# Attention scores issued in two groups instead of four, with the attention's and the gates' steps placed in other slots

## The chip, the cores and the metric

The kernel runs on one core of a Trainium2 chip. The time is device microseconds from launch to end on that core. The core has five engines that work from their own queues in program order: TensorE (PE in the profile; its weight loads are PEld), VectorE (DVE), ScalarE (ACT), GpSimd (POOL) and SyncE (SP), which issues most of the loads.

## The reference, cut to what matters

One decoder layer for a sequence of 256 positions of width 1024, all in float32:

```
proj  = x @ W_in                  -> [q | k | v | B | C | h | gate_attn | gate_conv]
y_att = causal attention(q, k, v) @ W_att      (8 heads of 64, rotary on the first 16 dims)
y_cnv = (B * causal_dwconv3(C * h)) @ W_cnv
mix   = (sigmoid(g_att) * y_att + sigmoid(g_cnv) * y_cnv) @ W_o
x     = LayerNorm(alpha * x + mix)
u     = causal_dwconv3(x @ W_up);  f = (silu(u_gate) * u_val) @ W_down
x     = LayerNorm(alpha * x + f)
```

With 256 positions there is one key block, so the block-sparse attention is plain causal attention over 256 keys. The change concerns the attention only, and the order in which it is mixed with the projections that come after q, k and v.

## The kernel before, in words

Each float32 operand is split into a high and a low part (fp32r), and a product is formed from three matmuls (high-high, high-low, low-high). Weights come as one packed stream: SyncE loads chunks of 1 MB into three buffers `raw`; ScalarE copies a unit of a chunk to its high part `wh` (`split_h`, L192) and VectorE subtracts it to get the low part `wl` (`split_l`, L197). There are nine buffers of each.

q, k and v come first. After them 22 units of weights for h, c, b (twice) and the 16 gates follow, two by two (`two_units`, L664). TensorE runs the wide part of each unit (`cols_wide`, L333: eight matmuls of 512 columns) and, after the second of a pair, the narrow parts of both (`cols_narrow`, L340: 16 matmuls of 256 columns). The result of each unit stands in one of four PSUM banks `acc`, in two halves that have to be summed: ScalarE copies one half to SBUF and VectorE adds the other (`conv_sum_act` L596 and `conv_sum_dve` L600 for h, c, b; `gate_sum_act` L648 and `gate_sum_dve` L652 for the gates).

The attention is spread over these units. Work of the attention and of the convolution is put beside unit `u` by `at(u, part, f)`, and `slot(u)` (L479) issues it: first the matmuls of the unit, then the lists "pe" and "act", then `split_h` of the weights five units ahead, `split_l` four units ahead, then the list "dve". Every engine keeps this order in its own queue, so an instruction that waits holds up all that stands behind it on its engine. `C0` is the first of these units (h); c starts at C0+2, b at C0+4, the second h, c, b at C0+6, C0+8, C0+10, and the gates at C0+12.

The steps for one pair of heads `p` (of four), with their slots before the change:

| step | what it does | slot |
|---|---|---|
| `scores` (L397, L405) | 12 matmuls q times k on half the array each (64 rows), the two heads side by side, into two PSUM banks `ps` | C0+4+3p |
| `masked` (L408, L413) | VectorE adds the mask, scales, and takes the row maxima; L416 negates them | C0+5+3p |
| `exps` (L419, L424) | ScalarE: four exponentials with row sums | C0+6+3p |
| `normalize` (L428) | VectorE: reciprocal and four products | C0+7+5p |
| `probs_T` (L436) | six transposes on TensorE into two banks `ps` | C0+8+5p |
| `probs_h`, `probs_l` (L445, L448) | ScalarE and VectorE split each head's result, a slot apart | C0+9+5p, C0+10+5p |
| `attend` (L451) | six matmuls with v; needs both parts of both heads from its second matmul on | C0+11+5p |
| `attend_h`, `attend_l` | split of the result | C0+12+5p |

There are four `ps` banks, used in turn by the transposes of q and k (`qk_transpose`, slot C0+2, read by `qk_h` and `qk_l` in C0+3), the scores, `probs_T` and `attend`. The masked scores have two buffers (tag "pr"), so pair 2 takes over that of pair 0 when pair 0's transposes are done. The convolution's steps `conv1` to `conv4` (L602 to L627) stand beside the units at L630.

Of the kernel before, what the change touches and what calls it, by code (L numbers as in the profile page):

```python
# [8 lines left out]
F32 = mybir.dt.float32  # L9
# [6 lines left out]
P = 128  # L16
# [4 lines left out]
HD = 64  # L21
# [116 lines left out]
def layer_kernel(ctx: ExitStack, tc: tile.TileContext, x, wpack, cpack, ln1_g, ln1_b, ln2_g, ln2_b, out):  # L138
    nc = tc.nc

    cst = ctx.enter_context(tc.tile_pool(name="cst", bufs=1))
    big = ctx.enter_context(tc.tile_pool(name="big", bufs=1))
# [10 lines left out]
    def ps_bank(name):  # L153
        return ps_pool.tile([P, 512], F32, tag="ps", name=name)

    def scratch(shape, name, bufs=None, tag="scr"):
        return tmp.tile(shape, F32, tag=tag, name=name, bufs=bufs or 6)
# [5 lines left out]
    chunks, plan_units, U = plan()  # L163
# [24 lines left out]
    def split_h(u):  # L188

        issue_dma(units[u]["chunk"] + RAW_BUFS - 1)  # L190
        alloc(u, "h", "wh")
        nc.scalar.activation(units[u]["h"], raw_of(u), AF.Copy)  # L192

    def split_l(u):

        alloc(u, "l", "wl")
        nc.vector.tensor_tensor(units[u]["l"], raw_of(u), units[u]["h"].bitcast(F32), op=ALU.subtract)  # L197
# [161 lines left out]
    qkT = big.tile([P, 2, KT, S], F32R, tag="b16", name="qkT")  # L359
# [34 lines left out]

    SB, SM, PR = {}, {}, {}

    def scores(p):  # L397

        SB[p] = [ps_bank(f"s{p}_{j}") for j in range(2)]
        for t in range(2):  # L400
            n = (t + 1) * P
            for a, b in ((0, 0), (0, 1), (1, 0)):
                for j in range(2):
                    hs = slice(j * HD, (j + 1) * HD)
                    nc.tensor.matmul(SB[p][j][:, t * 256:t * 256 + n], qkT[hs, a, p, t * P:(t + 1) * P],  # L405
                                     qkT[hs, b, 4 + p, 0:n], start=a + b == 0, stop=a == 1)

    def masked(p):  # L408
        st = tmp.tile([P, 16], F32, tag="st", name=f"st{p}", bufs=4)
        sm = scratch([P, 2, 384], f"sm{p}", tag="pr", bufs=2)  # L410
        for t in range(2):
            for j in range(2):
                nc.vector.tensor_tensor_reduce(  # L413
                    out=sm[:, j, PCOL[t]], in0=SB[p][j][:, t * 256:t * 256 + P * (t + 1)], in1=MASK[t], scale=SCALE,
                    scalar=-3.0e38, op0=ALU.add, op1=ALU.max, accum_out=st[:, 2 * t + j:2 * t + j + 1])
        nc.vector.tensor_scalar(st[:, 4:8], st[:, 0:4], -1.0, None, op0=ALU.mult)  # L416
        SM[p] = (sm, st)
# [56 lines left out]
    def at(u, part, f, *a):  # L474
        beside.setdefault(u, {}).setdefault(part, []).append((f, a))
# [3 lines left out]
    def slot(u, products=None):  # L479


        if products:
            products()
        mine = beside.pop(u, {})
        for f, a in mine.get("pe", []) + mine.get("act", []):
            f(*a)
        while done["h"] <= u + LA + 1:
            if units[done["h"]]["h"] is None:
                split_h(done["h"])
            done["h"] += 1  # L490
        while done["l"] <= u + LA:
            if units[done["l"]]["l"] is None:
                split_l(done["l"])
            done["l"] += 1
        for f, a in mine.get("dve", []):
            f(*a)
# [9 lines left out]
    C0 = U[(OFF_H, 0)]  # L506
    for t in range(2):
        at(C0 + t, "dve", rope, t)
    for g2 in (0, 2, 1, 3):
        at(C0 + 2, "pe", qk_transpose, g2)  # L510
        at(C0 + 3, "act", qk_h, g2)
        at(C0 + 3, "dve", qk_l, g2)
    for p in range(4):
        at(C0 + 7 + 5 * p, "dve", normalize, p)
    for p in range(4):
        s = C0 + 4 + 3 * p
        at(s, "pe", scores, p)
        at(s + 1, "dve", masked, p)
        at(s + 2, "act", exps, p)
        s = C0 + 7 + 5 * p  # L520
        at(s + 1, "pe", probs_T, p)
        for j in range(2):
            at(s + 2 + j, "act", probs_h, p, j)
            at(s + 2 + j, "dve", probs_l, p, j)
        at(s + 4, "pe", attend, p)
        at(s + 5, "act", attend_h, p)
        at(s + 5, "dve", attend_l, p)


    def x_split(k):  # L530
# [96 lines left out]
    def conv4_dve(pr):  # L627
        low(yT[:, 1, 2 * pr:2 * pr + 2, :], CB["t", pr], yT[:, 0, 2 * pr:2 * pr + 2, :])

    for pr, (c1, c2, c3, c4) in enumerate(((6, 10, 11, 13), (13, 16, 18, 21))):  # L630
        at(C0 + c1, "dve", conv1, pr)
        at(C0 + c2, "act", conv2_act, pr)
        at(C0 + c2, "dve", conv2_dve, pr)
        at(C0 + c3, "dve", conv3, pr)
        at(C0 + c4, "act", conv4_act, pr)
        at(C0 + c4, "dve", conv4_dve, pr)
        for nm, off in (("h", OFF_H), ("c", OFF_C), ("b", OFF_B)):
            for e in range(2):
                at(U[(off, pr)] + e + 2, "act", conv_sum_act, nm, pr, e)
                at(U[(off, pr)] + e + 2, "dve", conv_sum_dve, nm, pr, e)  # L640


    GB = {}
# [13 lines left out]
    for j in range(16):  # L657
        u = U[("g", 0)] + j
        at(max(u + 3, C0 + 17), "act", gate, j)
        at(u + 2, "act", gate_sum_act, j)  # L660
        at(u + 2, "dve", gate_sum_dve, j)


    def two_units(u, names):  # L664
        banks = []
        for e in range(2):
            banks.append(acc_bank(names[e]))
            slot(u + e, lambda: cols_pair(u + e, e == 1, banks, xT))
        return banks
# [9 lines left out]
    for e in range(2):  # L679
        slot(U[("g", 0)] + 16 + e)  # L680
# [20 lines left out]
    for half in range(2):  # L701
        for e in range(2):
            ua, uc = U[("ao", half)] + e, U[("co", half)] + e
            for n in range(2):
                i = half * 4 + e * 2 + n
                if i > 1:
                    mix_hl(i - 2)
                ahead(uc + n - 1)
                bank = ps_bank(f"y{i}")
                unit_cols(uc, bank[:, 256:512], yT[:, 0], yT[:, 1], n * P)  # L710
                unit_cols(ua, bank[:, 0:256], aT[:, 0], aT[:, 1], n * P)
                if i == 0:
                    slot(uc + n)
                mix(i, bank)
# [139 lines left out]
    rows = {}  # L854
# [191 lines left out]
```

## Time and profile before

| what | value |
|---|---|
| median of 3 runs | 368.86 us (368.48 to 370.68) |
| profiled execution, its own time | 369.0 us |
| its span, first to last instruction | 367.1 us |
| mean granted TensorE clock | 0.997 |
| busy: TensorE, VectorE, ScalarE, GpSimd | 358.0, 294.9, 217.0, 7.0 us |
| data read, share of the span's time | 68.24 MB, 189 GB/s with what is written |

The page gives each engine's busy time and the chain of work that ended last; the order of time (timeline) gives each engine's instructions with start and length in us, merged where equal ones follow each other, with the idle time before them and what ended it in brackets. A length reaches to the end of the last one; since instructions overlap at their ends, the distance between two starts is the better price of one step. In the chain, times of TensorE are those of the ends, some 0.1 us later than the starts in the order of time.

### The profile page before, as it was taken

Reading aid. Unit: us, or ns where it says so; the run is one execution under the profiler, and the core shown is the slowest. Engines: PE = TensorE matmul, PEld = TensorE weight load, DVE = VectorE, ACT = ScalarE, POOL = GpSimd, SP = SyncE. Lnnn points to the kernel's source line nnn. Section 1 sums busy time; section 2 is a strip of 40 time slices with the busy share of each in tenths; the row PEclk is TensorE's granted clock in tenths of the full one; section 3 lists DMA queues with packets and bytes.
Section 4 is the critical chain, followed back from the end, with each engine's and each line's share of the span. In section 5 each row is a group of like instructions: output and inputs, shape, how many; then the busy total and the mean of one; then the engine's idle time right before and its main releaser. Section 6 shows DMA issues by size and latency. Waiting matters only on the chain.

```text
span 367.1 us, 5335 instructions
## 1 busy us (share of the span) xinstructions
PE 358.0 (98%) x2022; PEld 312.2 (85%) x2022; DVE 294.9 (80%) x510; ACT 217.0 (59%) x372; POOL 7.0 (2%) x26
## 2 busy tenths in 40 slices
PE   8999999999999999999999999999999999999991
PEld 7888888888888899988888888888888888888891
DVE  4696887788895679869769988987869696999784
ACT  4685776747867654634266666575657566676300
POOL 2000000000000000102000000000000000000000
PEclk9999999999999999999999999999999999999998
DMA  7978565333853634596360835448182645662011
GB/s 263 356 292 318 180 225 211 114 114 129 331 214 130 221 124 137 190 357 224 124 223 12 341 121 221 153 193 309 46 334 90 254 140 204 228 237 108 0 59 57
DMA packets 11241, 69.63 MB, mean 190 GB/s; under 512 B 1232, under 2 KB 1616, under 8 KB 4176
## 3 DMA queue, kind: packets, MB, share of 16 engines
q1 hardware_dynamic: 10496, 67.00, 50.0%
q0 software_dynamic: 576, 2.10, 1.8%
q8 instruction: 16, 0.26, 0.3%
q10 hardware_dynamic: 144, 0.20, 0.1%
q14 instruction: 9, 0.07, 0.1%
HBM read 68.24 MB, written 1.05 MB: 189 GB/s over the span
## 4 chain that ended last, share of the span: by engine, by line
PE 97%; DVE 1%; DMA 1%; DVEq 0%; SPq 0%; issue 0%
PE pb L333 20%; PE pb L340 10%; PE g L333 8%; PE d L305 5%; PE d L306 5%; PE d L307 5%; PE g L340 4%; PE q L555 3%; PE k L555 3%; PE v L555 3%; PE b L333 2%; PE y L326 2%; PE y L325 2%; PE y L324 2%; PE c L333 2%; PE o L307 2%
## 5 line engine op out<-in xcount | busy, mean ns | idle before, releaser
L197 DVE TENSOR_TENSOR wl<-raw,wh 128x1024 fp32r<-128x1024 f32 x90 | 109.8, 1221 | 23.3 <-ACT wh L192 22.7
L192 ACT ACTIVATE wh<-raw 128x1024 fp32r<-128x1024 f32 x90 | 94.5, 1055 | 22.7 <-DMA raw<-in_wpack 22.6
L333 PE MATMUL pb<-x1T,wh 128*128 128x512 f32 x320 | 76.2, 390 | 0.0
L333 PEld LDWEIGHTS pb<-x1T,wh 128*128 128x128 f32 x320 | 59.7, 188 | 12.1
L220 DVE TENSOR_TENSOR wl<-raw,wh 128x1024 fp32r<-128x1024 f32 (+1 forms) x38 | 38.0, 1037 | 7.4 <-ACT wh L219 7.1
L340 PEld LDWEIGHTS pb<-x1T,wl 128*128 128x128 f32 x320 | 41.0, 191 | 1.6
L340 PE MATMUL pb<-x1T,wl 128*128 128x256 f32 x320 | 41.5, 283 | 0.0
L219 ACT ACTIVATE wh<-raw 128x1024 fp32r<-128x1024 f32 (+1 forms) x38 | 32.9, 904 | 14.3 <-DMA raw<-in_wpack 8.5
L333 PE MATMUL g<-xT,wh 128*128 128x512 f32 x128 | 31.4, 393 | 0.0
L305 PE MATMUL d<-wh,f 128*128 128x512 f32 x80 | 31.3, 391 | 0.0
L306 PE MATMUL d<-wl,f 128*128 128x512 f32 x80 | 31.3, 391 | 0.0
L307 PE MATMUL d<-wh,f 128*128 128x512 f32 x80 | 31.1, 389 | 0.0
L333 PEld LDWEIGHTS g<-xT,wh 128*128 128x128 f32 x128 | 23.3, 188 | 4.5
L807 ACT ACTIVATE fb<-pb 128x512 f32<-128x512 f32 x20 | 11.9, 595 | 23.8 <-PE pb L340 23.8
L825 DVE SCALAR_TENSOR_TENSOR fc<-fb,consts,fc 128x254 f32<-128x254 f32 x40 | 19.3, 484 | 1.4
L823 DVE SCALAR_TENSOR_TENSOR fc<-fb,consts,fc 128x255 f32<-128x255 f32 x40 | 19.1, 478 | 0.0
L817 ACT ACTIVATE fc<-fb,consts 128x256 f32<-128x256 f32 x40 | 17.9, 496 | 0.4 <-DVE fb L811 0.4
L307 PEld LDWEIGHTS d<-wh,f 128*128 128x128 f32 x80 | 15.0, 188 | 3.2
L305 PEld LDWEIGHTS d<-wh,f 128*128 128x128 f32 x80 | 15.1, 189 | 2.7
L306 PEld LDWEIGHTS d<-wl,f 128*128 128x128 f32 x80 | 15.1, 189 | 2.6
L340 PEld LDWEIGHTS g<-xT,wl 128*128 128x128 f32 x128 | 16.4, 191 | 0.6
L340 PE MATMUL g<-xT,wl 128*128 128x256 f32 x128 | 16.6, 283 | 0.0
(183 smaller groups left out, 606.1 us busy)
## 6 DMA issues: line engine op xcount, KB each, us to landing
raw<-in_wpack SPq DMA_DIRECT2D x55, 1024.0 KB, 4.9
raw<-in_wpack SPq DMA_DIRECT2D x6, 896.0 KB, 5.5
xr<-in_x SPq DMA_DIRECT2D x1, 1024.0 KB, 7.6
ln<-in_ln_g POOLq DMA_DIRECT2D x2, 512.0 KB, 5.6
ln<-in_ln_b POOLq DMA_DIRECT2D x2, 512.0 KB, 6.2
raw<-in_wpack SPq DMA_DIRECT2D x3, 256.0 KB, 3.4
raw<-in_wpack SPq DMA_DIRECT2D x1, 512.0 KB, 5.8
out<-x SPq DMA_DIRECT2D x2, 256.0 KB, 2.1
```

The costliest lines, as they stand in the source:

```text
L192: nc.scalar.activation(units[u]["h"], raw_of(u), AF.Copy)
L197: nc.vector.tensor_tensor(units[u]["l"], raw_of(u), units[u]["h"].bitcast(F32), op=ALU.subtract)
L219: nc.scalar.activation(h, src, AF.Copy)
L220: (eng or nc.vector).tensor_tensor(l, src, h.bitcast(F32), op=ALU.subtract)
L305: nc.tensor.matmul(o, ah, bh, start=start, stop=False)
L306: nc.tensor.matmul(o, ah, bl, start=False, stop=False)
L307: nc.tensor.matmul(o, al, bh, start=False, stop=stop)
L333: nc.tensor.matmul(bank, un["h"][:, k, :], b[:, k].rearrange("p a s -> p (a s)"), start=k == 0, stop=False)
L340: nc.tensor.matmul(bank[:, 0:S], un["l"][:, k, :], b[:, k, 0], start=False, stop=k == nk - 1)
L555: nc.tensor.matmul(banks[m][t], (xl if p == 2 else xh)[:, k, t * P:(t + 1) * P], wl if p == 1 else wh, start=k == 0 and p == 0, stop=k == ...
L823: nc.vector.scalar_tensor_tensor(c[:, 1:S], pb[:, a * S:a * S + S - 1], w_ffn(1, j), c[:, 1:S], op0=ALU.mult, op1=ALU.add)
L825: nc.vector.scalar_tensor_tensor(c[:, 2:S], pb[:, a * S:a * S + S - 2], w_ffn(0, j), c[:, 2:S], op0=ALU.mult, op1=ALU.add)
```

## The change

- `scores` takes a list of pairs and issues the matmuls of all of them in one group, first the query half t = 0 for each pair, then t = 1. Pairs 0 and 1 are issued in slot C0+4, pairs 2 and 3 in C0+9. The number and the shapes of the matmuls stay.
- The masked scores of pairs 2 and 3 stand in a tile of their own (`sm23`), which takes the place of q and k (tag "rows"), not in the two buffers of pairs 0 and 1.
- The slots of the steps are written out pair by pair: masked C0+5, 7, 10, 12; exps C0+6, 8, 11, 13; normalize C0+8, 14, 17, 21; probs_T C0+11, 15, 19, 23; probs_h and probs_l one and two slots after probs_T, attend three, attend_h and attend_l four. attend ends in slot C0+26, as before.
- `slot` has a new list "first", which it issues between `split_h` and `split_l`. `conv_sum_dve` and `gate_sum_dve` move into it from "dve", so that they stand ahead of the slot's `split_l` in VectorE's queue.
- conv2 of the first h, c and b moves from C0+10 to C0+9; of the second, conv1 moves from C0+13 to C0+14 and conv4 from C0+21 to C0+20.

```
--- before.py
+++ after.py
@@ -394,20 +394,24 @@
 
     SB, SM, PR = {}, {}, {}
 
-    def scores(p):
-
-        SB[p] = [ps_bank(f"s{p}_{j}") for j in range(2)]
+    def scores(ps):
+
+        for p in ps:
+            SB[p] = [ps_bank(f"s{p}_{j}") for j in range(2)]
         for t in range(2):
             n = (t + 1) * P
-            for a, b in ((0, 0), (0, 1), (1, 0)):
-                for j in range(2):
-                    hs = slice(j * HD, (j + 1) * HD)
-                    nc.tensor.matmul(SB[p][j][:, t * 256:t * 256 + n], qkT[hs, a, p, t * P:(t + 1) * P],
-                                     qkT[hs, b, 4 + p, 0:n], start=a + b == 0, stop=a == 1)
+            for p in ps:
+                for a, b in ((0, 0), (0, 1), (1, 0)):
+                    for j in range(2):
+                        hs = slice(j * HD, (j + 1) * HD)
+                        nc.tensor.matmul(SB[p][j][:, t * 256:t * 256 + n], qkT[hs, a, p, t * P:(t + 1) * P],
+                                         qkT[hs, b, 4 + p, 0:n], start=a + b == 0, stop=a == 1)
 
     def masked(p):
         st = tmp.tile([P, 16], F32, tag="st", name=f"st{p}", bufs=4)
-        sm = scratch([P, 2, 384], f"sm{p}", tag="pr", bufs=2)
+        if p == 2:
+            SM["late"] = big.tile([P, 2, 2, 384], F32, tag="rows", name="sm23")
+        sm = scratch([P, 2, 384], f"sm{p}", tag="pr", bufs=2) if p < 2 else SM["late"][:, p - 2]
         for t in range(2):
             for j in range(2):
                 nc.vector.tensor_tensor_reduce(
@@ -477,6 +481,7 @@
     done = {"h": 0, "l": 0}
 
     def slot(u, products=None):
+
 
 
         if products:
@@ -488,6 +493,8 @@
             if units[done["h"]]["h"] is None:
                 split_h(done["h"])
             done["h"] += 1
+        for f, a in mine.get("first", []):
+            f(*a)
         while done["l"] <= u + LA:
             if units[done["l"]]["l"] is None:
                 split_l(done["l"])
@@ -510,21 +517,20 @@
         at(C0 + 2, "pe", qk_transpose, g2)
         at(C0 + 3, "act", qk_h, g2)
         at(C0 + 3, "dve", qk_l, g2)
-    for p in range(4):
-        at(C0 + 7 + 5 * p, "dve", normalize, p)
-    for p in range(4):
-        s = C0 + 4 + 3 * p
-        at(s, "pe", scores, p)
-        at(s + 1, "dve", masked, p)
-        at(s + 2, "act", exps, p)
-        s = C0 + 7 + 5 * p
-        at(s + 1, "pe", probs_T, p)
+
+    at(C0 + 4, "pe", scores, (0, 1))
+    at(C0 + 9, "pe", scores, (2, 3))
+    for p, (m, e, n, tr, av) in enumerate(((5, 6, 8, 11, 14), (7, 8, 14, 15, 18), (10, 11, 17, 19, 22), (12, 13, 21, 23, 26))):
+        at(C0 + m, "dve", masked, p)
+        at(C0 + e, "act", exps, p)
+        at(C0 + n, "dve", normalize, p)
+        at(C0 + tr, "pe", probs_T, p)
         for j in range(2):
-            at(s + 2 + j, "act", probs_h, p, j)
-            at(s + 2 + j, "dve", probs_l, p, j)
-        at(s + 4, "pe", attend, p)
-        at(s + 5, "act", attend_h, p)
-        at(s + 5, "dve", attend_l, p)
+            at(C0 + tr + 1 + j, "act", probs_h, p, j)
+            at(C0 + tr + 1 + j, "dve", probs_l, p, j)
+        at(C0 + av, "pe", attend, p)
+        at(C0 + av + 1, "act", attend_h, p)
+        at(C0 + av + 1, "dve", attend_l, p)
 
 
     def x_split(k):
@@ -627,7 +633,7 @@
     def conv4_dve(pr):
         low(yT[:, 1, 2 * pr:2 * pr + 2, :], CB["t", pr], yT[:, 0, 2 * pr:2 * pr + 2, :])
 
-    for pr, (c1, c2, c3, c4) in enumerate(((6, 10, 11, 13), (13, 16, 18, 21))):
+    for pr, (c1, c2, c3, c4) in enumerate(((6, 9, 11, 13), (14, 16, 18, 20))):
         at(C0 + c1, "dve", conv1, pr)
         at(C0 + c2, "act", conv2_act, pr)
         at(C0 + c2, "dve", conv2_dve, pr)
@@ -637,7 +643,7 @@
         for nm, off in (("h", OFF_H), ("c", OFF_C), ("b", OFF_B)):
             for e in range(2):
                 at(U[(off, pr)] + e + 2, "act", conv_sum_act, nm, pr, e)
-                at(U[(off, pr)] + e + 2, "dve", conv_sum_dve, nm, pr, e)
+                at(U[(off, pr)] + e + 2, "first", conv_sum_dve, nm, pr, e)
 
 
     GB = {}
@@ -658,7 +664,7 @@
         u = U[("g", 0)] + j
         at(max(u + 3, C0 + 17), "act", gate, j)
         at(u + 2, "act", gate_sum_act, j)
-        at(u + 2, "dve", gate_sum_dve, j)
+        at(u + 2, "first", gate_sum_dve, j)
 
 
     def two_units(u, names):
```

## The prediction

> **What bounds the kernel now.** I read the page's busy shares first, then its chain, then the sums over two long stretches, and only then the order of time of TensorE, VectorE and ScalarE around the attention (38 to 100 us). From the page:
>
> ```profile
> PE 358.0 (98%) x2022; PEld 312.2 (85%) x2022; DVE 294.9 (80%) x510; ACT 217.0 (59%) x372; POOL 7.0 (2%) x26
> ...
> PE 97%; DVE 1%; DMA 1%; DVEq 0%; SPq 0%; issue 0%
> ```
>
> Two stretches that cover nearly the whole span (length, then busy time of each engine):
>
> ```profile
> 5.00:182.00 177.00, 177.00 (x1035) 154.88 (x1036) 140.80 (x266) 109.06 (x199) 3.95 (x6) 1.00 0.60 216
> 182.00:359.00 177.00, 177.00 (x957) 153.76 (x957) 148.60 (x233) 106.66 (x173) 0.55 (x1) 1.00 0.46 170
> ```
>
> TensorE is busy for 354 us without a hole, at a granted clock of 1.00. So two things alone can move the time: what TensorE itself needs, and a wait that comes new into its queue. A wait there is lost for good, since no hole later gives it back; time saved on another engine brings nothing.
>
> **What TensorE saves.** The change issues the same 48 score matmuls in two groups and not four. The chain shows a group with its neighbours (start, length), two pieces of a common block, and two early pieces for a rival below:
>
> ```profile
> 4.78 2.33 PE q L555 x6
> ...
> 13.94 1.36 PE q L555 x6
> ...
> 53.16 0.89 PE s L405 x12
> 54.04 2.05 PE b L333 x8
> ...
> 58.00 3.65 PE h L333 x16
> 61.66 1.91 PE h L340 x16
> ```
>
> A group costs 0.89, and the eight wide matmuls behind it take 2.05 where sixteen of h take 3.65, so eight 1.83: 1.11 in all. Inside a group the matmuls run two at a time. These rows of TensorE's order of time, from several narrow windows, show starts, each row with what is left of the group:
>
> ```profile
> 51.15 2.00 PE L333 MATMUL b<-xT,wh 128*128 128x512 f32 x8
> ...
> 53.36 0.56 PE L405 MATMUL s<-qkT 64*128 64x128 f32 x6
> ...
> 53.47 0.57 PE L405 MATMUL s<-qkT 64*128 64x256 f32 x6
> ...
> 53.97 2.12 PE L333 MATMUL b<-xT,wh 128*128 128x512 f32 x8
> ...
> 66.91 2.08 PE L333 MATMUL c<-xT,wh 128*128 128x512 f32 x8
> ...
> 77.43 0.40 PE L305 MATMUL av<-vpt 128*128 128x512 f32 x1
> ```
>
> Twos start 0.11 apart (53.36, 53.47). A second pair of heads in the same group adds six such steps, 0.66, in place of 1.11: 0.45 saved, twice, 0.90. Against it, the transposes of pair 1 stood just ahead of a score group and now stand ahead of wide matmuls, which are then 0.08 longer (66.91 against 51.15). Net -0.8. Bounds: no saving at all (0), and at most the entries and exits of all four groups (four times 0.45, 1.8); I take 0.8, as only two groups go.
>
> **What the re-spread order does to VectorE and ScalarE.** These are the rows that price it, VectorE first (a price is the distance to the next start where two rows follow each other):
>
> ```profile
> 47.49 2.47 DVE L216 TENSOR_TENSOR qkT<-qkt,qkT 128x512 fp32r<-128x512 f32 x4
> 49.88 0.41 DVE L600 TENSOR_TENSOR ch<-h,ch 128x256 f32<-128x256 f32 x1
> ...
> 71.50 0.55 DVE L216 TENSOR_TENSOR vpt<-ptp,vpt 128x384 fp32r<-128x384 f32 x1
> 71.97 1.91 DVE L617 SCALAR_TENSOR_TENSOR ct<-z,consts,ct 128x256 f32<-128x256 f32 x4
> 73.79 0.42 DVE L600 TENSOR_TENSOR cc<-c,cc 128x256 f32<-128x256 f32 x1
> 74.13 1.22 DVE L197 TENSOR_TENSOR wl<-raw,wh 128x1024 fp32r<-128x1024 f32 x1
> 75.26 0.28 DVE L413 CUSTOM_DVE_ANT_0 sm<-s,mask 128x128 f32<-128x128 f32 x1
> ...
> 76.49 0.17 DVE L416 TENSOR_SCALAR st<-st 128x4 f32<-128x4 f32 x1
> 76.56 0.68 DVE L622 TENSOR_TENSOR ct<-cb,ct 128x512 f32<-128x512 f32 x1
> 77.17 0.41 DVE L600 TENSOR_TENSOR cc<-c,cc 128x256 f32<-128x256 f32 x1
> ...
> 78.63 0.17 DVE L430 RECIPROCAL st<-st 128x4 f32<-128x4 f32 x1
> ...
> 79.76 0.85 DVE L216 TENSOR_TENSOR aT<-av,aT 64x256 fp32r<-64x256 f32 x2
> ```
>
> ```profile
> 48.21 0.41 ACT L596 ACTIVATE ch<-h 128x256 f32<-128x256 f32 x1
> ...
> 55.51 0.40 ACT L424 ACTIVATE sm<-sm,st 128x128 f32<-128x128 f32 x1 [1.27 <-DVE st L416]
> ...
> 57.28 0.36 ACT L596 ACTIVATE cb<-b 128x256 f32<-128x256 f32 x1
> 57.55 1.05 ACT L192 ACTIVATE wh<-raw 128x1024 fp32r<-128x1024 f32 x1
> 58.50 0.37 ACT L596 ACTIVATE cb<-b 128x256 f32<-128x256 f32 x1
> ...
> 70.22 0.47 ACT L446 ACTIVATE vpt<-ptp 128x384 fp32r<-128x384 f32 x1
> 70.59 0.90 ACT L611 ACTIVATE ct<-z,consts 128x256 f32<-128x256 f32 x2
> ...
> 82.59 0.62 ACT L625 ACTIVATE yT<-ct 128x512 fp32r<-128x512 f32 x1
> 83.11 0.37 ACT L596 ACTIVATE cb<-b 128x256 f32<-128x256 f32 x1
> ...
> 95.20 1.28 ACT L655 ACT_TABLE_LOAD   x1
> 96.50 1.31 ACT L655 ACTIVATE gates<-gs,consts 128x256 f32<-128x256 f32 x3
> ```
>
> Prices on VectorE: a sum (ch, cc, cb) 0.34, a low split wl 1.13, masked 1.30 (its maxima are ready 1.40 after its start), normalize 1.13, conv2 1.82, conv3 0.61, conv1 the same as an estimate (both are one 128x512 product), probs_l 0.47, the four qkT lows 2.39. On ScalarE: exps 1.77, a sum 0.27 (ready after 0.37), wh 0.95, conv4 0.52. For a handover between the two I allow 0.03.
>
> No piece of work is added, but the list "first" puts each sum ahead of the slot's low split on VectorE, and ScalarE does that sum behind the exponentials of its slot. So VectorE, which used to do a split and go on while ScalarE was in the exponentials, now stands at the sum until they are done; queued behind it are the splits, masked, normalize and probs_l. That makes a closed chain: masked(p), exps(p), ScalarE's sum, VectorE's sum, the next slots' work, masked(p+1). I follow it in the order that the built program shows.
>
> - Start: slot C0+3. The sum of ch waits for ScalarE until 48.62; then sum 0.34, wl 1.13, four qkT lows 2.39, two slots' sums and splits 2.94: masked(0) at 55.45.
> - Round 0: maxima 1.40, exps 1.77, sum 0.37, handovers 0.06: VectorE goes on at 59.05. Two sums, two splits, conv1: 3.55. masked(1) at 62.60.
> - Round 1: 3.60 more, 66.20. Three sums, three splits, normalize(0), conv2: 7.36. masked(2) at 73.56.
> - Round 2: 77.16. Two sums, two splits, conv3, probs_l(0,0): 4.02. masked(3) at 81.18.
> - Round 3: 3.60, and conv4 0.52 ahead of the sum: 85.30. Sum and split 1.47: probs_l(0,1) starts at 86.77 and ends at 87.32 (0.55).
>
> attend(0) needs that last one from its second matmul on. When is TensorE there? Wide matmuls resume behind the first group at 53.97 + 0.66 = 54.6; rest of the b block 2.05 + 1.91; h and c blocks 5.56 each (3.65 + 1.91): 69.7. The second group, 0.89 + 0.66: 71.3; the b block with its 0.22: 77.0; six transposes of 128 columns, 0.11 each like the scores' steps, and their 0.08: 77.8; g block 5.56, eight wide 1.83: 85.2; second matmul 0.23 (3.65 / 16) later, 85.4. So TensorE stands 87.3 - 85.4 = 1.9 us at slot C0+14. Before, the same probs_l ended at 72.05 and attend came at 77.43: 5.4 us of cover, which this order uses up.
>
> Next, attend(1): from its transposes to its second matmul TensorE has 0.66 + 0.08 + 5.56 + 1.83 + 0.23 = 8.4. The other side: first three transposes some 0.5 with their latency, then on ScalarE probs_h 0.37, conv2 0.8, sum 0.27, wh 0.95, probs_h 0.37, table load 1.3, three gates 1.31, sum 0.37, then VectorE's sum, split, probs_l 2.0: 8.2. About even; I take 0 and up to 0.5. attend(2) and (3) have neither table load nor conv2, so some 2 us of cover.
>
> **What costs nothing, and its cover.** The group of pairs 0 and 1 fills all four score banks, so its seventh matmul (the fourth two, at 53.47) needs the last qkT low, at 50.12 + 2.47 = 52.6: 0.9 of cover; beyond it TensorE would stand. The second group needs masked(1), at 64.0, by 69.7. The masked scores of pairs 2 and 3 stand where q and k were: q and k are read for the last time by the transposes, whose lows are done by 52.6, long before 73.6, and x1, which takes the place next, comes behind the last attend. The low splits come later, but with much in hand: C0+13's, for one, ends at 70.4 and is used from 77.8 + 3.65 = 81.4. SP's order is the same, but the buffers that its loads wait for come free with the later splits, the first at 50.2; a load takes 4.9:
>
> ```profile
> raw<-in_wpack SPq DMA_DIRECT2D x55, 1024.0 KB, 4.9
> ```
>
> It lands at 55.1, and ScalarE first reads it at 60.1 (exps from 56.9, two sums, one wh). Nothing of POOL's queue moves.
>
> **Sum.** -0.8 + 1.9 = +1.1 on the profiled execution (369.0), so 370.1; the median of the runs shown is 368.86, which gives 370.0.
>
> **Rivals.**
> - The cover holds (another engine's idle time takes it up): VectorE is idle for 36 us of the first stretch and ScalarE for 68. Then only the saving is left, 368.1. Against it: the chain above is made of waits for each other, not of busy time.
> - Slower by over 1%: the place is attend(1), where both sides are even. If the new waits for the sums lengthen each round between two attends, the stall comes again at attend(1) to (3). It decides from 3.7 + 0.8 = 4.5 us of stall in all, 2.6 more than I count, 0.9 for each of three; then 372.6 or more. Against it: the later rounds have no exponentials in them.
> - The stall costs clock too. The first six q matmuls, before which TensorE had stood, took 2.33 where later ones take 1.36: +1.0 if that happens again, so 371.0. The Trainium skill, TensorE: Matmul & The Clock Gate, section Part 1: The HAM clock gate, has the clock halved only after an idle window of about 3.4 us; by that rule this stall is too short, and no row of before shows a stall in the middle that would test it.
>
> **How the numbers follow.** A stall of 0.8 to 3.0 us: 0.70; the forecast is its 370.0, range 368.9 to 371.2 (the chain is 39 us of some forty instructions, and 3% on it is 1.2). Cover holds: 0.14. Clock lost: 0.06. Over 1%: 0.06. Unknown: 0.04. To leave out at most two in ten, the range reaches down to the case of full cover, and up past the clock's: 368.0 to 371.5. A difference within 1% is about what a measurement of this kernel cannot tell from no change; by these cases it is slower 0.06, faster 0.01, same 0.93.
>
> **What would show it.** In the profile after: score rows of 24 matmuls, about 1.6 long, two in number; TensorE idle once for some 1.7 us near 85.5, ended by VectorE's vpt row; VectorE idle in front of the sums, ended by ScalarE, near 46, 57, 64, 75 and 83. Right on time but with no idle TensorE, the chain is wrong; idle at attend(1) to (3) as well, the second rival. I am wrong altogether if the wide matmuls themselves start to wait for splits or banks.

## The result and the profile after

The median after is 371.37 us (369.72 to 372.34, 18 runs) against 368.78 us (368.12 to 370.68, 18 runs) for the kernel before on the same chip: a ratio of 1.0063 [1.0049, 1.0077]. The change makes the kernel slower by 0.6%. The forecast was 370.0 us, or 1.1 us more; 2.6 us came.

The page after, busy time and shares of the chain:

```profile
PE 357.6 (97%) x2022; PEld 311.5 (85%) x2022; DVE 293.4 (80%) x510; ACT 217.0 (59%) x372; POOL 7.0 (2%) x26
...
PE 84%; DVE 9%; ACT 3%; DMA 2%; issue 1%; SPq 1%; DVEq 0%
```

TensorE has the same work, but the chain that ends last now leaves it for VectorE and ScalarE. All waits of TensorE in the profile after (total, times, longest):

```profile
PE av L306 <- DVE vpt L216: 1.9, 1, 1.9
PE warm L234 <- DVE zeros L224: 1.0, 1, 1.0
```

The second row is the start and stands in both kernels. The first is the new one: attend's second matmul waits for the low part of the transposed probabilities (`probs_l`). The order of time of VectorE, ScalarE and TensorE after shows how it comes about:

```profile
48.14 0.43 DVE L606 TENSOR_TENSOR ch<-h,ch 128x256 f32<-128x256 f32 x1 [2.22 <-ACT ch L602]
...
54.94 0.28 DVE L417 CUSTOM_DVE_ANT_0 sm<-s,mask 128x128 f32<-128x128 f32 x1
...
58.53 0.42 DVE L606 TENSOR_TENSOR cb<-b,cb 128x256 f32<-128x256 f32 x1 [2.20 <-ACT cb L602]
...
62.08 0.28 DVE L417 CUSTOM_DVE_ANT_0 sm<-s,mask 128x128 f32<-128x128 f32 x1
...
73.05 0.28 DVE L417 CUSTOM_DVE_ANT_0 sm<-s,mask 128x128 f32<-128x128 f32 x1
...
80.66 0.28 DVE L417 CUSTOM_DVE_ANT_0 sm<-s,mask 128x128 f32<-128x128 f32 x1
...
84.78 0.42 DVE L606 TENSOR_TENSOR cb<-b,cb 128x256 f32<-128x256 f32 x1 [2.72 <-ACT cb L602]
...
86.25 0.55 DVE L216 TENSOR_TENSOR vpt<-ptp,vpt 128x384 fp32r<-128x384 f32 x1
```

```profile
83.37 0.49 ACT L428 ACTIVATE sm<-sm,st 128x256 f32<-128x256 f32 x1
...
83.86 0.61 ACT L631 ACTIVATE yT<-ct 128x512 fp32r<-128x512 f32 x1
84.39 0.36 ACT L602 ACTIVATE cb<-b 128x256 f32<-128x256 f32 x1
```

```profile
52.57 1.66 PE L407 MATMUL s<-qkT 64*128 64x128 f32 x24
54.16 2.12 PE L333 MATMUL b<-xT,wh 128*128 128x512 f32 x8
...
84.61 0.39 PE L305 MATMUL av<-vpt 128*128 128x512 f32 x1
86.86 0.50 PE L306 MATMUL av<-vpt 128*128 128x512 f32 x1 [1.86 <-DVE vpt L216]
87.19 0.40 PE L307 MATMUL av<-vpt 128*128 128x512 f32 x1
...
99.64 0.39 PE L305 MATMUL av<-vpt 128*128 128x512 f32 x1
100.02 0.50 PE L306 MATMUL av<-vpt 128*128 128x512 f32 x1
```

Read the last round backwards: probs_l at 86.25 stands behind a split (84.78 to 86.25 with the sum), the sum behind ScalarE's half of it at 84.39, and that behind the exponentials and conv4. VectorE stood idle for 2.72 us ahead of it; TensorE pays 1.86.

**A better ruler than the span.** This profiled execution took 370.07 us, only 1.1 more than the one of before, but that mixes two things: its first h matmul started at 37.74, before's at 38.26. Between executions of one kernel this start wanders (37.3 to 40.6 in those recorded here). From the first y matmul on all kernels agree: 57.56 to 57.67 us to the next block and 180.3 from there to the end. So I compare the stretch from the first h matmul to the first y matmul, which holds the whole attention. The rows show the stretch, its length and the busy time of TensorE, its loads, VectorE, ScalarE and GpSimd; before, after, and a later execution of after:

```profile
38.26:129.27 91.01, 91.01 (x561) 79.71 (x560) 73.43 (x158) 64.06 (x133) 0.00 (x0) 1.00 0.52 186
```

```profile
37.74:130.43 92.69, 90.83 (x562) 79.58 (x560) 70.80 (x156) 64.04 (x134) 0.00 (x0) 1.00 0.47 171
```

```profile
37.78:132.00 94.22, 92.37 (x561) 80.75 (x560) 70.79 (x156) 63.99 (x134) 0.00 (x0) 0.98 0.47 168
```

The stage grew by 1.68 us in the first profile and by 3.21 in the other, the same kernel, at a granted clock of 0.98 in place of 1.00. So there were two questions: which part of the change makes the wait, and where the second 1.5 us come from.

### The profile page after: what moved, and what is told of

It is laid out like the page before. It is cut to its first block, busy times and chain, and to the rows that moved or that the text cites. A ratio compares the mean times of both kernels' runs of the same rounds, so it can differ in the third digit from the quotient of the medians.

```text
span 368.3 us, 5318 instructions
## 1 busy us (share of the span) xinstructions
PE 357.6 (97%) x2022; PEld 311.5 (85%) x2022; DVE 293.4 (80%) x510; ACT 217.0 (59%) x372; POOL 7.0 (2%) x26
## 4 chain that ended last, share of the span: by engine, by line
PE 84%; DVE 9%; ACT 3%; DMA 2%; issue 1%; SPq 1%; DVEq 0%
PE pb L333 20%; PE pb L340 10%; PE g L333 6%; PE d L305 5%; PE d L306 5%; PE d L307 5%; PE g L340 4%; DVE wl L197 3%; PE k L561 3%; PE v L561 3%; PE q L561 2%; PE y L326 2%; PE y L325 2%; PE y L324 2%; PE o L307 2%; PE o L306 2%
## 5 line engine op out<-in xcount | busy, mean ns | idle before, releaser
L817 DVE TENSOR_TENSOR fb<-pb,fb 128x512 f32<-128x512 f32 x20 | 13.7, 686 | 3.7 <-ACT fb L813 3.5
```

## The experiments

Theories. A: the list "first" alone makes the wait, because VectorE's sum then stands in front of the splits while ScalarE's half of that sum stands behind the exponentials. B: the new slots or the grouped scores make it. For the rest, C: the wait costs clock as well; D: something else in the changed order is slower. The kernel before had these medians on the same chips: 369.02 us beside the first four runs, 368.88 beside the next four, 369.36 (one run) beside the last three.

**The changed kernel again** (no edit).

> The changed kernel once more, unaltered, with a second profile. My theory: in every execution TensorE stands about 2.0 us in the attend of pair 0 (2.02 in the first profile, with 0.11 behind it) and 0.2 to 0.3 in that of pair 1, which less the 0.8 saved in the score groups gives +1.6 between the q, k, v stage and the end. The runs lie further above the kernel before than that (medians 371.37 and 368.78, 2.6 apart), and spread more (369.7 to 372.3 against mostly 368.1 to 369.5). Theory for the rest: after the stall some executions lose clock for a while; then slow runs show a lower granted clock (0.988) and a profile that falls on one shows matmul steps of about 0.43 us for 512 columns behind the stall. Rival for the rest: the stall itself is longer in some executions, with the clock unchanged; then a second profile shows more than 2.0 us at the same place.

371.93 us (369.87 to 372.78), ratio 1.0061 [1.0039, 1.0084]: the result repeats. Two of its 11 runs lie below 370.4; in the first comparison it was 6 of 18 below 370.7, and the other 12 at 371.0 to 372.3. The profiled execution (370.99) had a stage of 92.67 and the whole clock, but a late start (38.68).

**The sums back behind the splits**, everything else of the change kept:

```
-                at(U[(off, pr)] + e + 2, "first", conv_sum_dve, nm, pr, e)
+                at(U[(off, pr)] + e + 2, "dve", conv_sum_dve, nm, pr, e)
...
-        at(u + 2, "first", gate_sum_dve, j)
+        at(u + 2, "dve", gate_sum_dve, j)
```

> The changed kernel with the sums back in the list dve, behind the slot's split and attention work; groups of scores, slots and the buffer stay. My theory (the sums ahead of the splits make VectorE wait for the exponentials, and this wait reaches the attend of pair 0): no idle TensorE in the attends, probs_l of pair 0 done by about 82, 3 us ahead of TensorE; the 0.8 saved in the score groups is left, so about 368.0, ratio 0.998 to the kernel before. Rival (the re-spread slots themselves, with masked and exps of pair 3 just ahead of probs_l of pair 0, cost the time): TensorE still stands 1 to 2 us there, 369.5 to 371.

368.12 us (367.27 to 370.07), ratio 0.9974 [0.9956, 0.9991]. This version beats both kernels. VectorE's and TensorE's order of time and the stage:

```profile
80.67 0.55 DVE L216 TENSOR_TENSOR vpt<-ptp,vpt 128x384 fp32r<-128x384 f32 x1
```

```profile
84.46 0.39 PE L305 MATMUL av<-vpt 128*128 128x512 f32 x1
84.69 0.39 PE L306 MATMUL av<-vpt 128*128 128x512 f32 x1
```

```profile
37.59:127.83 90.24, 90.24 (x561) 79.70 (x560) 73.86 (x158) 64.53 (x134) 0.00 (x0) 1.00 0.52 187
```

probs_l is done at 81.2, 3.5 us before TensorE needs it. The stage is 0.77 shorter than before's: that is the grouped scores with nothing against them. B is out: the new slots and the groups make no wait.

**The list "first" alone, in the kernel before.**

```
+        for f, a in mine.get("first", []):
+            f(*a)
         while done["l"] <= u + LA:
...
-                at(U[(off, pr)] + e + 2, "dve", conv_sum_dve, nm, pr, e)
+                at(U[(off, pr)] + e + 2, "first", conv_sum_dve, nm, pr, e)
...
-        at(u + 2, "dve", gate_sum_dve, j)
+        at(u + 2, "first", gate_sum_dve, j)
```

> The kernel before with one part of the change alone: the sums issued ahead of the slot's low split on VectorE. Score groups, slots and buffers as before. My theory: the sum stands behind the exponentials here too; worked through with the same prices TensorE comes to stand some 0.4 us at the transposes of pair 1 (their normalize ends near 84.4, where TensorE is at 84.0) and 1.6 to 1.8 us at the attend of pair 1, 2 us in all: 370.8, ratio 1.005. Rival (only the re-spread slots cost the time): same as before, 368.8, with no idle TensorE.

371.94 us (371.7 to 374.47), ratio 1.0083 [1.0055, 1.0111]: the list alone makes the kernel slower, also with the old slots. TensorE's waits there, and one of VectorE's ahead of a sum:

```profile
PE av L306 <- DVE vpt L216: 1.4, 1, 1.4
...
PE ptp L440 <- DVE sm L434: 0.7, 1, 0.7
```

```profile
84.14 0.42 DVE L602 TENSOR_TENSOR cb<-b,cb 128x256 f32<-128x256 f32 x1 [2.74 <-ACT cb L598]
```

The wait at attend, there that of pair 1, was expected; the one of pair 2's transposes for normalize was not, and the time came out 1.1 us above the 370.8 expected. The stage is 94.20 in that execution, at a granted clock of 1.00: the list costs 3.19 there. By TensorE's starts, counted from the first h matmul, 0.55 of it arises at pair 1's transposes and the scores behind them (0.4 was expected), 1.69 at the attend of pair 1 and 0.95 at pair 2's transposes. With the new slots and groups the list costs 2.45 (92.69 without clock loss, against 90.24 without the list). So the new slots don't cause the harm; by these profiles they ease it a little.

**The list kept, but ScalarE's half of the sum ahead of the exponentials.**

```
-        for f, a in mine.get("pe", []) + mine.get("act", []):
+        for f, a in mine.get("sum", []) + mine.get("pe", []) + mine.get("act", []):
...
-                at(U[(off, pr)] + e + 2, "act", conv_sum_act, nm, pr, e)
+                at(U[(off, pr)] + e + 2, "sum", conv_sum_act, nm, pr, e)
```

> The changed kernel, with ScalarE's copies for the sums of h, c and b issued ahead of the slot's exponentials and probs_h, not behind them; VectorE's sums stay ahead of the low splits. My theory (VectorE's sum costs time only because ScalarE's half of it stands behind the exponentials): probs_l of pair 0 done near 82, no idle TensorE in the attend of pair 0, about 368.0, ratio 0.997 to the kernel before, like the run with the sums last. Rival (a sum ahead of the split is harmful by itself): TensorE still stands 1 us or more there, 370 or more.

368.16 us (367.7 to 370.08), ratio 0.9985 [0.997, 1.0]. attend's first two matmuls start at 85.08 and 85.31 without a wait; probs_l is done before:

```profile
82.58 0.55 DVE L216 TENSOR_TENSOR vpt<-ptp,vpt 128x384 fp32r<-128x384 f32 x1
```

VectorE's sum may stand first; what hurts is that it waits for an instruction that its producer does last. A is shown from three sides: taken away, alone, and with the producer moved. A little of the harm stays: the stage is 90.52, 0.28 more than with the sums last. This version moved the sums of h, c and b only. The gates' sums still stand as in the changed kernel, one of them waits ahead of the last probs_l of pair 1, and the second matmul of attend(1) comes 0.38 behind the first (97.96 to 98.34) and not 0.23:

```profile
96.26 0.42 DVE L658 TENSOR_TENSOR gs<-g,gs 128x256 f32<-128x256 f32 x1 [0.37 <-ACT gs L654]
```

**Four score groups in the changed kernel**, in slots C0+4, 5, 9 and 10.

```
-    at(C0 + 4, "pe", scores, (0, 1))
-    at(C0 + 9, "pe", scores, (2, 3))
+    for p, c in enumerate((4, 5, 9, 10)):
+        at(C0 + c, "pe", scores, (p,))
```

> The changed kernel with the scores in four groups again, in slots C0+4, C0+5, C0+9 and C0+10. My theory: the stall ends at a time set by VectorE and ScalarE, so 0.9 us more of TensorE work ahead of it only shortens the stall, from 2.0 to about 1.1; the time stays within 0.3 us of the changed kernel. Rival (TensorE's work and its stall add up): 0.9 us slower than the changed kernel, with the stall at 2.0.

370.29 us (369.83 to 372.88), ratio 1.0046 [1.0025, 1.0066]. TensorE and the stage:

```profile
85.56 0.39 PE L305 MATMUL av<-vpt 128*128 128x512 f32 x1
87.03 0.50 PE L306 MATMUL av<-vpt 128*128 128x512 f32 x1 [1.08 <-DVE vpt L216]
```

```profile
37.90:130.58 92.68, 91.59 (x562) 79.67 (x560) 70.84 (x156) 64.29 (x133) 0.00 (x0) 1.00 0.47 171
```

TensorE is busy for 0.76 longer than after, it waits 0.78 less, and the stage is as long (92.68 against 92.69). The saving of the groups is real and is wholly given back as waiting, because VectorE's chain, which ends the wait, doesn't get shorter. So far this is as expected, but the median is 1.6 us below that of the changed kernel in the same comparison (371.93), where at most 0.3 was expected: 7 of 10 runs lie at 369.8 to 370.3. So the longer wait costs something that the same stage length in these two profiles does not show. That points to C: all ten runs have a mean granted clock of 0.992 to 0.996, while 4 of the 11 of the changed kernel have 0.988 to 0.991.

**A longer wait**: VectorE writes one low split once more, and in a second kernel three times more, ahead of the late probs_l.

```
+    def low_again(u):
+        nc.vector.tensor_tensor(units[u]["l"], raw_of(u), units[u]["h"].bitcast(F32), op=ALU.subtract)
+
+    for _ in range(1):
+        at(C0 + 13, "dve", low_again, C0 + 16)
```

> The changed kernel with one low split done twice on VectorE (the same unit, the same values), just ahead of the last probs_l of pair 0. It lengthens TensorE's stall by 1.13, from 2.0 to about 3.2 us. Theory of a stall that costs its length and no more: about 1.1 us over the changed kernel, its fast group at 371.2 where that of the changed kernel is at 370.1, granted clock as there. Theory that the stall costs clock in some executions: more of them lose it, a median 1.5 to 2.5 us over the changed kernel's, clock 0.988 in most, and matmul steps of 0.43 us for 512 columns behind the stall in the profile.

> The same with three splits more: a stall of 2.0 + 3.4 = 5.4 us. Theory of a stall that costs its length: 3.4 over the changed kernel, fast group at 373.5, clock as there. Theory that it costs clock: every execution loses a further 1.5 to 1.7 us, about 375.2 and more, and the profile shows the 0.43 us steps behind the stall.

One split more: 373.27 us (371.01 to 374.79), ratio 1.0117 [1.0087, 1.0148]. Three: 375.29 us (374.67 to 375.9), ratio 1.0176 [1.0151, 1.0202]. The waits became 3.0 and 5.5. The first one's profile, TensorE alone (stretch, length, busy, granted clock, share of DMA, GB/s):

```profile
84.00:88.07 4.07, 1.79 (x8) 1.00 0.00 0
88.07:94.90 6.83, 6.12 (x18) 0.50 0.43 154
94.90:98.00 3.10, 3.10 (x24) 1.00 0.80 314
```

From 88.07 on, before the wait ends (at 88.78), the granted clock is 0.50 for 6.83 us. With three splits it was 3.41 us. So a wait in the middle can cost clock, and a longer one doesn't cost proportionately more. Not every execution pays: of the six runs with one split more, five have a mean granted clock of 0.984 to 0.991 and take 372.9 to 374.8 us, and the sixth has 0.996 and takes 371.0, which is what was expected of a wait that costs its length alone (371.2).

**The changed kernel, four more profiled executions**, to see whether its own wait does that.

> The changed kernel unaltered, for one more profile. Theory of lost clock: if this execution is one of those at 371 or more with TensorE started as early as in the first profile, matmuls behind the stall of pair 0's attend take 0.43 us for 512 columns for some 1 to 3.4 us; if it is one at 370, they do not. Rival: a longer stall than 2.0 us.

> The changed kernel unaltered, one of three more looks. The longer stall of 3.0 us has shown half clock behind it (6.8 us of it); the changed kernel's own stall of 1.9 us has not in three profiles, of executions at 370.1, 370.3 and 371.0, while most executions lie at 371 to 373. Theory of lost clock: a look that falls on an execution of 371.6 or more with a normal start shows a stretch at half clock behind the stall, 0.43 us per 512 columns; a look at about 370 shows none. Rival: such an execution has the full clock there, and the time is lost elsewhere, in the start or in a longer stall.

> The changed kernel unaltered, the second of three more looks; as for the first.

> The changed kernel unaltered, the third of three more looks; as for the first.

370.27, 371.14, 371.72 and 371.99 us. The first has the wait (1.86) and no loss, and a stage of 92.64. The other three have the same wait (1.85) and a stage of 94.20 to 94.24. The order of time of TensorE in the execution of 370.27, then the same and the granted clock around the wait in that of 371.72:

```profile
87.10 0.50 PE L306 MATMUL av<-vpt 128*128 128x512 f32 x1 [1.86 <-DVE vpt L216]
...
88.01 2.02 PE L333 MATMUL g<-xT,wh 128*128 128x512 f32 x8
```

```profile
84.65 0.39 PE L305 MATMUL av<-vpt 128*128 128x512 f32 x1
86.89 0.50 PE L306 MATMUL av<-vpt 128*128 128x512 f32 x1 [1.85 <-DVE vpt L216]
...
87.93 3.46 PE L333 MATMUL g<-xT,wh 128*128 128x512 f32 x8
```

```profile
84.26:87.67 3.41, 1.56 (x8) 1.00 0.16 24
87.67:91.09 3.42, 3.42 (x11) 0.50 0.70 283
91.09:95.00 3.91, 3.91 (x30) 1.00 0.45 140
```

Eight wide matmuls that took 2.02 in the execution without loss take 3.46 here: for 3.41 us the clock is half. The stage is 1.55 longer for it. This is C, in the changed kernel itself; D has nothing left to explain in these profiles.

The mean granted clock of the other runs says how often it happens. 3.41 us at half clock lower the mean of a run of 370 us by 0.005. In 86 runs of the kernel before and of the versions with the sums last, with four groups, with the list alone and with ScalarE's half first, the mean lies between 0.992 and 0.996. Of the 29 runs of the changed kernel in two comparisons, 10 lie at 0.988 to 0.991 (371.3 to 372.8 us): these lost clock. 10 at 0.993 or more did not, since with 0.005 added they would lie above all the others, and 9 at 0.992 leave it open. Three of the ten without loss still took 371.0 to 372.0; a late start could explain them, but they were not profiled.

What decides between loss and none stays open. The changes of the granted clock lie on a grid of 3.41 us. In the three executions with loss the whole 1.85 us of idle time falls inside one interval of it (in the rows above 85.04 to 86.89 inside 84.26 to 87.67), and TensorE is busy for 1.56 us of that interval. In two of the three profiles of this kernel without loss (370.27 and 370.99) an interval's end, worked back from the drop of the clock after the last matmul, cuts the idle time, and no interval has less than 1.76 us of busy time. The first profile does not fit. There an interval ends at 86.86, just where the idle time ends (85.00 to 86.86), so by these rows (TensorE alone) it holds all of it, and yet the clock stayed whole:

```profile
83.45:86.86 3.41, 1.55 (x8) 1.00 0.00 0
86.86:90.28 3.42, 3.42 (x19) 1.00 0.88 280
```

Either the edge lies a little otherwise than these rows place it, or the share of idle time in one interval is not what decides. Neither was tried, nor at what share the clock would drop.

## Why the prediction was right, and where it was not

- **Bound by TensorE, new waits are lost for good**: right. The wait stays in the stage to the end, though VectorE is idle for 38 us between 5 and 182 us.
- **The saving of 0.8**: 0.77 measured with nothing in its way. But as a term of this kernel's sum it is no gain of time: without the two groups the wait is 0.78 shorter. The sum holds only because the forecast counted the earlier arrival of TensorE into the wait.
- **The closed chain**: right, step by step. The forecast had masked at 55.45, 62.60, 73.56 and 81.18 and probs_l at 86.77; measured are 54.94, 62.08, 73.05, 80.66 and 86.25, and with the 0.51 by which this execution began earlier 55.45, 62.59, 73.56, 81.17 and 86.76. TensorE was due at 85.4 and, shifted alike, came at 85.35.
- **The wait at attend(0), 1.9**: the second matmul came 2.25 behind the first, where 0.23 is usual: 2.02. Not counted: the step behind a released matmul is 0.33 (86.86 to 87.19) and not 0.23, another 0.11 (0.34 by the trace's nanoseconds).
- **attend(1), taken at 0, up to 0.5**: the second matmul there comes 0.38 behind the first, so 0.15, and 0.11 behind it. In sum 2.02 + 0.11 + 0.15 + 0.11 - 0.77 = 1.62, against the 1.68 of the stage and the +1.1 of the forecast.
- **Low splits, banks, loads, q and k's space at no cost**: right; TensorE has no other wait.
- **The step that failed: the rival "the stall costs clock too"**, given 0.06. Its mechanism is what happens in many executions: three of the four later profiles show it, by their mean clock at least 6 of the 18 runs had it, and 12 of 18 runs lie where it puts them, though a late start can put single runs there as well. It costs 1.55, not 1.0: the price had been taken from the start's first matmuls. The trace disagrees with the rule of the Trainium skill, TensorE: Matmul & The Clock Gate, section Part 1: The HAM clock gate, which I let speak against it: an idle window of about 3.4 us was not needed, 1.85 us of idle time was enough in three executions. The length of the window, 3.41 us, agrees, and so does that the window runs freely: in each of the six executions its ends fall at another place against the first h matmul.
- **The median**: 1.65 of stage without the loss, 3.2 with it, and a mixture of both in the runs, fits the measured 2.6; the share of runs with loss is known only within the bounds given above. The main case's own range (368.9 to 371.2) is missed by 0.2. That the time stayed inside the wide one (368.0 to 371.5) is luck in part: it reached past the clock's case, whose chance was put far too low.

## What to carry to other kernels

Before an instruction is moved up in an engine's queue, look at its producer's queue: where the producer does its part last, everything behind the consumer inherits that wait, and the two queues can lock into a chain that no busy share shows. A saving on an engine that then waits is given back in full; the two edits here were worth measuring apart, since the groups alone gain 0.8 us of stage and the list alone costs three to four times that. Price a wait of TensorE in the middle of full work with what its clock may lose behind it, and compare stages between two fixed instructions where the start of the program wanders.

## What the runs showed of the hardware

- TensorE's granted clock halves after 1.85 us of idle time, in some executions of one kernel and not in others; it stays at 0.50 for 3.41 us and costs 1.55 us here. With a wait of 3.0 us it stayed there for 6.83 us, with one of 5.5 us for 3.41 us (one profile each). Of the 16 runs of the two versions whose longest wait in this stage was 1.1 and 1.4 us, none has a mean granted clock below 0.992.
- Where the first matmul behind a wait is one of 512 columns, the next one starts 0.33 to 0.34 later instead of 0.23.
- The start of the first h matmul wandered between 37.3 and 40.6 us from execution to execution, while the changed kernel's stage from there to the first y matmul repeated to 0.05 us at a full clock (92.64 to 92.69).
